# Layer 0's FFN modulation vectors on VectorE in the output projection and the first FFN, in place of TensorE in the projections

## The chip, the cores and the metric

The kernel runs on one core of a Trainium2 chip. A core has five engines with their own instruction queues: TensorE (PE, matrix multiplies; PEld is its weight load), VectorE (DVE), ScalarE (ACT), GpSimd (POOL) and SyncE (SP, which here only issues DMAs). Each queue runs in order. The metric is the device time of one execution in microseconds (us), the median of several runs.

## The reference, cut to what matters

Two layers work on 1024 latent and 256 context tokens of width 1024, all in float32. Every layer is modulated by six vectors that come from a conditioning vector, one set for the latent and one for the context tokens:

```python
sc, scc = jax.nn.silu(c), jax.nn.silu(c_ctx)
for l in range(DEPTH):
    mod_l = jnp.split((sc @ ada_w[l] + ada_b[l])[:, None, :], 6, axis=-1)
    mod_c = jnp.split(scc @ ada_w[l] + ada_b[l], 6, axis=-1)
    h_lat = rms_norm(x, norm1_g[l]) * (1 + mod_l[1]) + mod_l[0]
    ...
    x = x + mod_l[2] * y_lat
    h = rms_norm(x, norm2_g[l]) * (1 + mod_l[4]) + mod_l[3]
    x = x + mod_l[5] * conv_ffn(h, ffn_w_up[l], ffn_conv_w[l], ffn_conv_b[l], ffn_w_down[l])
    ...
```

So vectors 0 and 1 are shift and scale of the mixer, 2 is its gate, and 3, 4 and 5 are shift, scale and gate of the FFN. `ada_w[l]` is 1024 x 6144. Layer 0's mixer is attention (12 heads) beside a gated convolution of width 31 over 512 channels; layer 1's is a long convolution beside a recurrence.

## The kernel before, in words

**Layout.** Activations lie transposed: 8 tiles of 128 channels by 1280 tokens (256 context, then 1024 latent). A dense product in float32 is made as three matmuls on halves of the numbers (`mm3`, L338 to L340): high by high, high by low, low by high. Weights come in units of 128 x 1024 (`wunit`): a DMA on SP into `wraw` (2 buffers), a cast to the high part `whi` on ACT (L331), and the low part `wlo` by a subtraction on POOL (L332), 3 buffers each.

**Modulation vectors, two ways.** Layer l's `adaw` lies in three sets s of two vectors each, and a set in four quarters j of 512 columns: s = 0 holds vectors 0 and 1, s = 1 holds 2 (j = 0, 1) and 3 (j = 2, 3), s = 2 holds 4 (j = 0, 1) and 5 (j = 2, 3). `ada_gen` makes a set on TensorE: for each of 8 row blocks k a DMA brings 128 x 1024 weights (two quarters), and two matmuls with `sc` (128 x 32, of which two columns are used) as weights add them up in one psum tile `adaps`, each quarter j in its own 32 columns of the array (L365); at the end a copy, four transposes (`adapt`, L374) and the addition of the bias (L379) write `modT`. `ada_vec` makes a set on VectorE: for each quarter and k a DMA of 128 x 512, then one multiply (L395) or multiply-add (in the helper `stt`, L1197) for each of the two conditionings into the accumulator `adacc`; after 8 k, tiny matmuls with ones (`adv`, L405) add over the partitions, and the bias is added in the helper `add` (L1193). `ada_vec` is a generator that yields its booked cost, 0.7 us for each multiply-add; a `Side` object (`side`) runs such generators in turn, and `side.run(us)` puts out as many of their instructions as that budget covers.

**Order.** The program is written in one order, and a scheduler arranges each engine's queue by a simulated timeline with the order of writing as priority; `later(n)` lowers the priority of what is written in it by n instructions.

**Layer 0's projections** (`layer0`, to about 380 us). Set 0 is made first. Then come, in this order, the gated halves of the convolution input for channel blocks 0 to 3 (`l0_conv`) and the attention inputs in five blocks (`l0_block`, ten token tiles each: matmuls, then ACT, DVE and POOL work on `z` and a DMA to memory). The convolution's taps are side work: 104 multiply-adds on DVE (L1197), and 8 taps each of blocks 0 and 1 as a scaled copy on ACT into a buffer `ctap` (L722) and an accumulating DMA issued from POOL (L723), which DVE adds at the end. With `later(400)`, behind block 0 and behind block 1, the TensorE form makes the sets s = 1 and s = 2 of layer 0, and its weight tiles take their turn in the same three `ctap` buffers (the class constant `ADA` says behind which steps).

**Attention** runs to about 984 us. **The output projection** (`project`, 984 to 1150) then splits the last three of ten input chunks (`load_split`, buffers `ysrc`), and computes the 8 output blocks m first for token tiles 0 and 1 (the context and half of the latent tokens), then for tile 2; each result is scaled by the gate and added to x on DVE, its squares are summed on ACT and POOL, and after a group TensorE, DVE and POOL make the norm's factor.

**The first FFN** (`ffn` and `build`, to about 2150): `ada_A` joins scale and gain; `norm_h` normalizes on DVE, ACT and POOL; then for each of 22 blocks f `up` makes value and gate, and `side.run(8.5)` puts out side work; after every second f from 2 on, `down` adds the products of two earlier blocks to x, scaled by vector 5 (`resid`, L869 and L872). The side work is layer 1's three sets by `ada_vec` (s = 0 for both conditionings, the others for the latent tokens alone) and the long convolution's filters (`filters`). What is left is put out ahead of the last `project`.

Of the kernel before, what the change touches and what calls it, by code (L numbers as in the profile page):

```python
# [17 lines left out]
P = 128  # L18
# [229 lines left out]
class Kern:  # L248
# [129 lines left out]
        for i, j in enumerate(js):  # L378
            nc.vector.tensor_tensor(out=dst[:, j], in0=src[:, i], in1=bias[:, j], op=ALU.add)  # L379

    def ada_vec(self, l, s, cs, wbuf, acc, psf, pool=None):


        nc = self.nc
        bias = self.col(f"adab{l}", 48, 2)
        for j in range(4):
            a = [acc(i) for i in range(len(cs))]
            for k in range(KD):
                w = wbuf()
                nc.sync.dma_start(out=w, in_=self.i["adaw"][l, s, k, j // 2][:, j % 2 * 512:j % 2 * 512 + 512])  # L390
                for i, c in enumerate(cs):
                    f = self.sc[:, k, c:c + 1]
                    if k == 0 or pool:
                        t = pool() if k else a[i]
                        (nc.gpsimd if pool else nc.vector).tensor_scalar(out=t, in0=w, scalar1=f, scalar2=None, op0=ALU.mult)  # L395
                        if k:
                            self.add(a[i], a[i], t, pool=True)
                    else:
                        self.stt(a[i], w, f, a[i])
                yield 0.7 * len(cs)  # L400
            ps = psf("adv")
            n = len(cs)
            for b in range(4):
                for i in range(n):
                    nc.tensor.matmul(ps[:, b * n + i:b * n + i + 1], lhsT=a[i][:, b * P:(b + 1) * P],  # L405
                                     rhs=self.ones[:, 0:1], start=True, stop=True)
            m = slice(s * 16 + 4 * j, s * 16 + 4 * j + 4)
            self.add(self.modT[l][:, m, cs[0]:cs[-1] + 1], ps[:, :4 * n].rearrange("p (b c) -> p b c", c=n),
                     bias[:, m, cs[0]:cs[-1] + 1])
# [81 lines left out]
                    nc.vector.scalar_tensor_tensor(out=lo, in0=t, scalar=b, in1=h.bitcast(F32),  # L491
                                                   op0=ALU.add, op1=ALU.subtract)

    def project(self, weights, hs, x, l, j, tts, accs, scratch=None, cuts=(-1,)):

        K = len(hs)
        pbs = []
# [3 lines left out]
        for group in (tiles[a:b] for a, b in zip(cuts, cuts[1:])):  # L501
            ss = [accs(n)[:, :t[1][1]] for n, t in enumerate(group)]
            for m in range(KD):
# [7 lines left out]
                for n, (i, (o, N, lat)) in enumerate(group):  # L511
# [4 lines left out]
                    xt = x[m][:, o:o + N]  # L516
                    self.stt(xt, out, self.mod(l, j, m, 1 - lat), xt)
                    sq[n] = self.ss_add(ss[n], xt, m, N, scratch, m == KD - 1)
            for n, (i, (o, N, lat)) in enumerate(group):
                pb = None  # L520
                if self.ns and i < 2:
# [34 lines left out]
    def layer0(self):  # L556
# [3 lines left out]
        with ExitStack() as sa:  # L560
# [44 lines left out]
            side = Side()  # L605
            self.od = [self.dr.tile([P, T], F32, name=f"od{c}") for c in range(10)]
            zs = [None] * 5
            ada = [(0, 1), (0, 2)]
            for blk, c in ((None, 0), (None, 1), (None, 2), (4, 3), (0, None), (1, None), (2, None), (3, None)):
                if blk is not None:  # L610
                    zs[blk] = self.l0_block(blk, h, c1, side)
# [1 line left out]
                    conv[c] = self.l0_conv(c, h, c1, c2, side, ready)  # L613
                if ada and (blk, c) in self.ADA:
                    with self.later(400):
                        self.ada_set(*ada.pop(0), lambda: c2.tile([P, UL], F32, name="adaw", tag="ctap", bufs=3), self.a_ps)
        if "z" in self.dbg:
            for b in range(5):
                for i in range(2):
# [16 lines left out]
        with ExitStack() as sc:  # L636
# [8 lines left out]
                return self.wunit(self.i["wo0t"][m // 4].rearrange("p m k c -> p (m k c)"))  # L645
            tail = unit_tail(0)
            ready = [unit(0)]
            hs = early + self.load_split(oh, [self.od[k] for k in order[7:]], T, (512, TC + 512, T), 2)
            for k in range(KD):
                nc.sync.dma_start(out=x[k], in_=self.i["xT"][k])  # L650

            def weights(m):
# [9 lines left out]
                def wk(i):  # L662
                    k = order[i]
                    if k < 8:
# [3 lines left out]
                return wk  # L668
            pbs = self.project(weights, hs, x, 0, 2, self.TT,
                               lambda n: oh.tile([P, 512], F32, name="ssacc", tag="ssacc", bufs=2),  # L670
                               lambda n: oh.tile([P, 512], F32, name=n, tag="ssq", bufs=2))
        self.oc.close()
        return x, pbs

    PTAPS = (8, 8, 0, 0)
    VCUT = 1300
    DEFER = ()
    ADA = ((None, 0), (None, 1))
    RB, RV, RC = 0.75, 2.0, 12.0

    def glu(self, c, g):
# [1204 lines left out]
def build(tc, ctx, ins, out, at, dbg=None, upto=None):  # L1886
# [14 lines left out]
    with ExitStack() as s:  # L1901
# [2 lines left out]
        k.fp = k.pool("fp", stack=k.fs)  # L1904
        k.norm_h(0, 1, x, hh, hl, k.TT, pbs)
        side = Side()
        for n in range(3):
            side.add(k.ada_vec(1, n, (0,) if n else (0, 1),
                               lambda: k.st.tile([P, 512], F32, name="adaw", tag="sq", bufs=3),
# [50 lines left out]
```

## Time and profile before

| | |
|---|---|
| median of 3 runs | 3833.98 us (3825.24 to 3834.63) |
| the profiled execution | 3841.95 us, its span 3839.9 us |
| mean granted TensorE clock | 0.963 |
| busy share of the span | PE 91%, PEld 76%, DVE 59%, POOL 35%, ACT 33% |
| chain that ended last | PE 71%, DVE 12%, issue 7%, ACT 4%, DMA 4%, POOL 3% |
| modulation weights loaded | 128 DMAs of 256 KB, 32 of 512 KB |

The profile shows one execution. Its time and its span differ by what lies ahead of the first and behind the last instruction. In the page's picture of the span in 40 slices a digit is the busy share in tenths. An arrow in a list of waits points to what ended the wait, with the total, the number of times and the longest. A row of the timeline has the start, the duration, the engine, the line, the operation, what it wrote and read, and its count. A matmul on whole float32 numbers (adaps, adv) stands as two records in the trace, one on the halves (L338 to L340) as one.

### The profile page before, as it was taken

How to read it: one execution, taken by the hardware profiler on the slowest of the kernel's cores; microseconds unless marked ns; L12 is line 12 of the kernel's file. 1: busy time of each engine (PE TensorE's matmuls, PEld its weight loads, DVE VectorE, ACT ScalarE, POOL GpSimd, SP SyncE). 2: the span in 40 equal slices, each digit the busy share in tenths (PEclk: the TensorE clock that was granted, in tenths of full speed). 3: DMA queues.
4: the chain of work that ended last, by engine and by line, in shares of the span. 5: the costliest groups of instructions: out<-in, count | busy, mean ns of one | idle time of the engine just before them, and what ended most of it. 6: DMA issues, size and time to landing. Idle time of an engine off the chain costs nothing.

```text
span 3839.9 us, 48138 instructions
## 1 busy us (share of the span) xinstructions
PE 3499.0 (91%) x18708; PEld 2918.8 (76%) x18708; DVE 2281.4 (59%) x2824; ACT 1257.2 (33%) x2175; POOL 1361.1 (35%) x1024
## 2 busy tenths in 40 slices
PE   6988688888899999999999899999777889999998
PEld 4768566666787888888888788977666778888886
DVE  5978456666226656655656688355697454343435
ACT  4134566666233111222222422222111342222222
POOL 3148242211262111122332554355566642222123
PEclk9999799999999999999999899999888999999999
DMA  5374111000322223212222377523345311111111
GB/s 205 114 184 105 56 57 32 21 24 20 106 83 85 86 92 101 75 56 71 79 78 69 122 212 203 146 89 103 114 143 196 121 61 50 50 43 51 44 55 55
DMA packets 202867, 351.12 MB, mean 91 GB/s; under 512 B 23504, under 2 KB 124432, under 8 KB 202640
## 3 DMA queue, kind: packets, MB, share of 16 engines
q1 hardware_dynamic: 172240, 311.22, 25.2%
q0 software_dynamic: 26496, 30.48, 3.7%
q10 hardware_dynamic: 3904, 6.36, 0.5%
q8 instruction: 147, 2.41, 0.3%
q14 instruction: 80, 0.66, 0.1%
HBM read 275.04 MB, written 62.39 MB: 88 GB/s over the span
## 4 chain that ended last, share of the span: by engine, by line
PE 71%; DVE 12%; issue 7%; ACT 4%; DMA 4%; POOL 3%; SPq 0%; DVEq 0%; ACTq 0%; POOLq 0%
PE dl L338 13%; PE dl L339 13%; PE dl L340 13%; PE pj L338 2%; PE pj L340 2%; PE pj L339 2%; PE pT L1048 2%; PE dc L338 2%; PE dc L340 2%; PE dc L339 2%; PE o L1062 1%; DVE pl L1053 1%; PE S L1009 1%; PE S L1010 1%; PE Bp L1570 1%
## 5 line engine op out<-in xcount | busy, mean ns | idle before, releaser
L332 POOL TENSOR_TENSOR wlo<-wraw,whi 128x1024 fp32r<-128x1024 f32 (+1 forms) x226 | 575.3, 2552 | 1214.7 <-ACT whi L331 1214.3
L339 PE MATMUL dl<-hl,whi 128*128 128x512 f32 x1920 | 759.4, 396 | 4.0 <-POOL hl L1193 3.4
L338 PE MATMUL dl<-hh,whi 128*128 128x512 f32 x1536 | 604.8, 394 | 9.3 <-DVE fc L1104 7.4
L340 PE MATMUL dl<-hh,wlo 128*128 128x512 f32 x1536 | 604.0, 393 | 0.0
L331 ACT CAST whi<-wraw 128x1024 fp32r<-128x1024 f32 (+1 forms) x226 | 225.0, 1005 | 867.0 <-PE dl L339 412.9
L339 PEld LDWEIGHTS dl<-hl,whi 128*128 128x128 f32 x1920 | 363.3, 189 | 84.0 <-POOL hl L1193 5.5
L1102 DVE SCALAR_TENSOR_TENSOR fc<-dl,cols,fc 128x1023 f32<-128x1023 f32 x84 | 107.5, 1279 | 407.8 <-ACT fc L1101 407.8
L338 PEld LDWEIGHTS dl<-hh,whi 128*128 128x128 f32 x1536 | 289.9, 189 | 73.8 <-issue 7.6
L340 PEld LDWEIGHTS dl<-hh,wlo 128*128 128x128 f32 x1536 | 289.8, 189 | 65.2 <-POOL wlo L332 0.7
L872 DVE SCALAR_TENSOR_TENSOR x<-dl,modT,x 128x1024 f32<-128x1024 f32 x160 | 204.3, 1278 | 115.0 <-PE dl L340 114.0
L338 PE MATMUL dl<-gs,whi 128*128 128x512 f32 x640 | 253.9, 397 | 9.2 <-DVE fc L1104 9.2
L340 PE MATMUL dl<-gs,wlo 128*128 128x512 f32 x640 | 250.5, 391 | 0.0
L339 PE MATMUL dl<-gs,whi 128*128 128x512 f32 x640 | 250.5, 391 | 0.0
L1053 DVE TENSOR_TENSOR pl<-pT,ph 128x512 fp32r<-128x512 f32 x252 | 167.8, 686 | 74.2 <-ACT ph L1052 73.7
L1048 PE MATMUL pT<-ident,p 128*128 128x128 f32 x1008 | 166.6, 288 | 44.8 <-DVE pl L1053 39.3
L1026 DVE TENSOR_REDUCE nm<-S 128x1 f32<-128x1280 f32 (+1 forms) x120 | 153.0, 1275 | 56.0 <-PE S L1010 53.5
L1052 ACT CAST ph<-pT 128x512 fp32r<-128x512 f32 x252 | 142.5, 586 | 131.3 <-PE pT L1048 130.3
L1062 PE MATMUL o<-ph,vs 128*128 128x256 f32 x504 | 144.8, 301 | 34.3 <-ACT ph L1052 20.3
L1048 PEld LDWEIGHTS pT<-ident,p 128*128 128x128 f32 x1008 | 120.6, 146 | 69.1 <-DVE pl L1053 54.1
L1197 DVE SCALAR_TENSOR_TENSOR conv<-u,cols,conv 128x1287 f32<-128x1287 f32 (+14 forms) x104 | 172.1, 1685 | 0.9
L1193 POOL TENSOR_TENSOR ot<-ot,rb 64x256 f32<-64x256 f32 x60 | 43.5, 725 | 332.2 <-DVE ot L1193 332.2
L338 PE MATMUL dl<-hl,whi 128*128 128x512 f32 x384 | 154.6, 404 | 1.7 <-ACT whi L331 0.8
(377 smaller groups left out, 8488.5 us busy)
## 6 DMA issues: line engine op xcount, KB each, us to landing
wraw<-in_wup SPq DMA_DIRECT2D x88, 512.0 KB, 3.6
adaw<-in_adaw SPq DMA_DIRECT2D x128, 256.0 KB, 2.8
wraw<-in_wdn SPq DMA_DIRECT2D x44, 512.0 KB, 3.6
adaw<-in_adaw SPq DMA_DIRECT2D x32, 512.0 KB, 4.5
df<-in_dftf POOLq DMA_DIRECT2D x64, 256.0 KB, 4.3
wraw<-in_w1f SPq DMA_DIRECT2D x24, 512.0 KB, 3.7
x<-in_xT SPq DMA_DIRECT2D x16, 640.0 KB, 9.4
spd<-so SPq DMA_DIRECT2D x68, 128.0 KB, 2.2
```

The costliest lines, as they stand in the source:

```text
L331: nc.scalar.copy(hi[:, :cols], raw[:, :cols])
L332: nc.gpsimd.tensor_tensor(out=lo[:, :cols], in0=raw[:, :cols], in1=hi[:, :cols].bitcast(F32), op=ALU.subtract)
L338: mm(out, lhsT=lh, rhs=rh, start=first, stop=False)
L339: mm(out, lhsT=lh, rhs=rl, start=False, stop=False)
L340: mm(out, lhsT=ll, rhs=rh, start=False, stop=last)
L872: nc.vector.scalar_tensor_tensor(out=xl, in0=pl, scalar=self.mod(l, j, m, 0), in1=xl, op0=ALU.mult, op1=ALU.add)
L1026: nc.vector.tensor_reduce(out=nm[:, i:i + 1], in_=s, op=ALU.max, axis=AX.X, negate=True)
L1048: nc.tensor.transpose(pt[:, (2 * a + i) * P:(2 * a + i + 1) * P], p[:, kc * P:(kc + 1) * P], self.ident)
L1052: nc.scalar.copy(ph, pt)
L1053: nc.vector.tensor_tensor(out=pl, in0=pt, in1=ph.bitcast(F32), op=ALU.subtract)
L1062: nc.tensor.matmul(o, lhsT=vs[:, kc], rhs=x[:, a * 256:a * 256 + 256], start=(kc == 0 and j == 0), stop=(kc == nk // P - 1 and j == 1))
L1197: self.nc.vector.scalar_tensor_tensor(out=out, in0=a, scalar=s, in1=b, op0=ALU.mult, op1=op)
```

## The change

Set s = 1 is made on TensorE only for j = 0, 1 (vector 2, the mixer's gate), behind block 0. Vectors 3 and 4 (s = 1, j = 2, 3 and s = 2, j = 0, 1) are made by `ada_vec` as side work of the output projection: 6.4 us of it after each of the blocks m = 0 to 6, and all that is left after m = 7 of the first group of token tiles; its weight tiles use the three buffers `sq`, its accumulators the two `ysrc`. Vector 5 (s = 2, j = 2, 3) is made by `ada_vec` as the first side work of the FFN, ahead of layer 1's sets, with accumulators in the buffers `tot` and `w3h`.

```diff
-    def ada_vec(self, l, s, cs, wbuf, acc, psf, pool=None):
+    def ada_vec(self, l, s, cs, wbuf, acc, psf, pool=None, js=(0, 1, 2, 3)):
...
-        for j in range(4):
+        for j in js:
...
-    def project(self, weights, hs, x, l, j, tts, accs, scratch=None, cuts=(-1,)):
+    def project(self, weights, hs, x, l, j, tts, accs, scratch=None, cuts=(-1,), side=None):
...
                     sq[n] = self.ss_add(ss[n], xt, m, N, scratch, m == KD - 1)
+                if side:
+                    side.run(self.OSIDE if m < KD - 1 else 1e9)
...
-            ada = [(0, 1), (0, 2)]
+            ada = [(0, 1)]
...
-                        self.ada_set(*ada.pop(0), lambda: c2.tile([P, UL], F32, name="adaw", tag="ctap", bufs=3), self.a_ps)
+                        self.ada_set(*ada.pop(0), lambda: c2.tile([P, UL], F32, name="adaw", tag="ctap", bufs=3), self.a_ps,
+                                     js=(0, 1))
...
             ready = [unit(0)]
+            side = Side()
+            for s, js in ((1, (2, 3)), (2, (0, 1))):
+                side.add(self.ada_vec(0, s, (0, 1),
+                                      lambda: self.st.tile([P, 512], F32, name="adaw", tag="sq", bufs=3),
+                                      lambda i: oh.tile([P, 512], F32, name="adacc", tag="ysrc", bufs=2),
+                                      self.s_ps, js=js))
...
-                               lambda n: oh.tile([P, 512], F32, name=n, tag="ssq", bufs=2))
+                               lambda n: oh.tile([P, 512], F32, name=n, tag="ssq", bufs=2), side=side)
...
+    OSIDE = 6.4
...
-    ADA = ((None, 0), (None, 1))
+    ADA = ((None, 0),)
...
         side = Side()
+        bufs = (lambda: k.st.tile([P, 512], F32, name="adaw", tag="sq", bufs=3),
+                lambda i: k.fp.tile([P, 512], F32, name="adacc", tag=("tot", "w3h")[i]), k.s_ps)
+        side.add(k.ada_vec(0, 2, (0, 1), *bufs, js=(2, 3)))
```

## The prediction, made before the change was timed

> **What bounds the kernel now.** I read the slices first, then the stretches that the change touches, then what TensorE (PE) and VectorE (DVE) wait for in them.
>
> ```profile
> PE   6988688888899999999999899999777889999998
> ```
>
> A slice is 96 us. PE is busy 80% or more almost everywhere, so time is won by taking work or waits from it, unless another engine stands right behind it. Then the stretches (the layer 0 projections end near 380 us, the output projection lies from 984 to 1150, the first FFN to 2085). After the length of the stretch stand the busy times of PE, of its weight loads, DVE, ACT and POOL, then PE's granted clock, the share of the DMA engines and GB/s:
>
> ```profile
> 140.00:190.00 50.00, 50.00 (x301) 32.20 (x300) 44.68 (x30) 9.09 (x15) 4.31 (x2) 1.00 0.61 182
> ...
> 280.00:340.00 60.00, 50.99 (x390) 49.77 (x389) 55.19 (x96) 29.08 (x156) 52.69 (x39) 0.94 0.58 131
> ...
> 60.00:380.00 320.00, 300.99 (x1887) 250.42 (x1886) 255.81 (x344) 102.32 (x417) 153.09 (x115) 0.96 0.46 122
> ...
> 1000.00:1083.00 83.00, 81.46 (x429) 69.52 (x430) 12.77 (x22) 19.84 (x32) 33.33 (x21) 0.97 0.24 77
> ...
> 1160.00:2085.00 925.00, 901.57 (x4623) 758.86 (x4622) 567.82 (x659) 216.20 (x244) 223.85 (x129) 0.99 0.26 80
> ```
>
> From 140 to 190 PE is the bound alone (50.00 of 50). From 280 to 340 it has gaps, and DVE (55.19 of 60) and GpSimd (POOL, 52.69) are fuller than it (50.99). In the output projection DVE is nearly empty, in the FFN it is 61% busy, and PE is nearly full in both. The chain that ended last, and the waits of PE and DVE in the projections, name the gaps:
>
> ```profile
> 230.97 9.39 DMA acc<-ctap
> 240.51 3.60 DMA adaw<-in_adaw
> ...
> 380.58 3.84 DMA zl<-zd
> ...
> PE adaps L365 <- DMA adaw<-in_adaw: 9.0, 3, 6.9
> ...
> DVE conv L1193 <- DMA acc<-ctap: 17.2, 2, 13.3
> DVE modT L379 <- PE adapt L374: 8.4, 1, 8.4
> ```
>
> The modulation weights (adaw) share three buffers, the tag ctap, with the convolution taps that leave by accumulating DMAs. PE waits 9.0 us for adaw that finds no buffer, and DVE 17.2 us for accumulations and 8.4 us for the modulation vector.
>
> **What goes from the projections.** Set (0,2) and half of set (0,1): of 32 pairs of modulation matmuls, 24.
>
> ```profile
> L365 PE MATMUL adaps<-adaw,sc 128*32 128x512 f32 x128 | 36.6, 619 | 9.0 <-DMA adaw<-in_adaw 9.0
> ...
> 181.05 0.28 PE L340 MATMUL qkv<-whi,hl 128*128 128x256 f32 x1
> 181.17 0.28 PE L338 MATMUL qkv<-whi,hh 128*128 128x256 f32 x1
> 181.38 1.05 PE L365 MATMUL adaps<-adaw,sc 128*32 128x512 f32 x4
> 182.36 0.38 PE L339 MATMUL qkv<-wlo,hh 128*128 128x256 f32 x1
> 182.58 0.28 PE L340 MATMUL qkv<-whi,hl 128*128 128x256 f32 x1
> ...
> 192.44 0.60 PE L374 MATMUL adapt<-ident,adasb 128*128 128x128 f32 x4
> ```
>
> A pair is four records (128 records are 32 pairs). From 181.17 to 182.58 are 1.41 us, in which two qkv matmuls at their pace of 0.12 also ran: a pair costs 1.17 us. 24 x 1.17 = 28.1 us, and 0.5 for one set's four transposes. The waits of PE on adaw, 9.0 us, all belong to set (0,2), which is gone. After the longest of them PE also ran slow:
>
> ```profile
> 227.45 1.92 PE L365 MATMUL adaps<-adaw,sc 128*32 128x512 f32 x4 [6.93 <-DMA adaw<-in_adaw]
> ...
> 233.52 0.36 PE L340 MATMUL qkl<-whi,hl 128*128 128x256 f32 x1
> ...
> 230.00:232.00 2.00, 2.00 (x11) 2.00 (x11) 0.00 (x0) 0.00 (x0) 1.02 (x2) 0.50 0.35 29
> ```
>
> The 6.1 us from 227.45 to 233.52, at a granted clock of 0.50, lost 3.0 us. If PE alone set the time, the gain would be 28.1 + 0.5 + 9.0 + 3.0 = 40.6 us.
>
> DVE stands behind it. In the 320 us from 60 to 380 it is busy 255.81; the idle time that the change can shorten is the 17.2 us (eight pairs fewer stand ahead of the first tap in the buffers) and the 8.4. The rest is the wait for the first convolution input, the tail after the last tap, and waits inside the blocks, which stay. So a stage set by DVE gains at most 25.6 us. Between 25.6 and 40.6 I take **29**, near the DVE end, because the last 60 us at 55.19 of 60 are what the whole stretch would look like. The transfers that go (24 of 512 KB) only make room, on SP's queue too. What is late next is the path from the projections over ACT and DVE to z.
>
> **What is added.** Six sets of accumulation: four in the output projection (shift and scale of the FFN), two in the first FFN ahead of layer 1's (its gate). The gate of the mixer stays with TensorE. Each set is 8 loads of 256 KB on SP, 2 multiplies and 14 multiply-adds on DVE, 8 tiny matmuls on PE, one addition. The first FFN does the same for layer 1 already:
>
> ```profile
> L1197 DVE SCALAR_TENSOR_TENSOR adacc<-adaw,sc,adacc 128x512 f32<-128x512 f32 x112 | 107.7, 980 | 1.6 <-DMA adaw<-in_adaw 0.9
> ...
> L395 DVE TENSOR_SCALAR adacc<-adaw,sc 128x512 f32<-128x512 f32 x16 | 12.8, 805 | 26.7 <-PE adv L405 24.6 <-DMA adaw<-in_adaw 2.2
> ...
> 1212.13 1.84 PE L405 MATMUL adv<-ones,adacc 128*128 128x1 f32 x16
> 1213.83 0.36 PE L338 MATMUL dc<-hh,whi 128*128 128x256 f32 x1
> 1214.03 0.28 PE L339 MATMUL dc<-hl,whi 128*128 128x256 f32 x1
> ...
> PE dl L338 <- DVE fc L1104: 16.5, 9, 7.4
> ```
>
> *PE:* 1213.83 - 1212.13 is 1.70 us, and the next step is 0.20 in place of 0.12: 1.78 us a set, 6 x 1.78 = **+10.7 us**. It lies on the path, since PE is full in both stages.
>
> *DVE in the output projection:* 2 x 0.805 + 14 x 0.980 = 15.3 us a set, 61 us for four, beside 12.8 us of its own between 1000 and 1083: 74 us in 83. A set can start when the matmuls of the one before have read its accumulators. The code asks for 6.4 us of side work after each of eight blocks m and books 11.2 for a set, so a set's matmuls stand behind every second block: one set in 2 x 83/8 = 21 us, against 15.3. That hides it, barely.
>
> ```profile
> L1197 DVE SCALAR_TENSOR_TENSOR adacc<-adaw,sc,adacc x112: 735/742/2897, 1171.0 to 1583.1; 128x512 f32<-128x512 f32 x112
> ...
> 1012.89 0.69 DVE L533 TENSOR_TENSOR yl<-ysrc,yh 128x512 fp32r<-128x512 f32 x1 [0.69 <-ACT yh L532]
> ...
> 1109.83 1.54 DVE L491 SCALAR_TENSOR_TENSOR hl<-nt,modT,hh 128x512 fp32r<-128x512 f32 x1
> ...
> 1150.59 0.16 DVE L451 TENSOR_SCALAR ms<-sums 128x4 f32<-128x4 f32 x1 [6.52 <-PE sums L448]
> ...
> 1245.71 0.15 DVE L1193 TENSOR_TENSOR modT<-adv,cols 128x8 f32<-128x8 f32 x1
> 1248.03 0.47 DVE L869 SCALAR_TENSOR_TENSOR x<-dc,modT,x 128x256 f32<-128x256 f32 x1
> ```
>
> The accumulators use the buffers of the split loads (yl), taken until 1013.6, while the first set's matmuls stand behind the second block, near 1021: the first set is the likely one to hold PE. The first norm, which now waits for shift and scale, ends at 1111 and is needed when the FFN starts after 1150; it may be 39 us late for nothing. Bounds: 0, and 14 us, four times the 3.4 by which 14 multiply-adds at 0.980 exceed 14 at the shortest, 0.735. I take **+3**, nearer to the FFN, where no set holds PE.
>
> *FFN:* the gate's two sets take the place of layer 1's first two sets, which have the same form. The second of those was written at 1245.71, and the first residual addition, which now waits for it, ran at 1248.03: just in time. Behind that addition on DVE stand further ones, and PE waits for the psum that they free; a late set would cost some 2 us. Everything later in the side work moves back by two sets, 30.6 us of DVE. DVE has 357 us idle there, but PE already loses 16.5 us to it in 925; scaled by 30.6/568 that is 0.9: **+1** (0 to 7.4, the longest one wait). At its end:
>
> ```profile
> 2080.00:2120.00 40.00, 39.49 (x214) 33.40 (x212) 20.17 (x33) 14.05 (x22) 13.63 (x8) 1.00 0.17 53
> ...
> L1381 DVE TENSOR_TENSOR hfb<-hps,dec x32: 671/678/694, 1712.8 to 2067.0; 128x512 f32<-128x512 f32 x32
> ...
> L1193 DVE TENSOR_TENSOR fsd<-hfb x64: 406/424/4189, 1714.0 to 2068.7; 128x256 f32<-128x256 f32 x64
> ```
>
> The code's own costs gave the side work 22 x 8.5 = 187 us for 181; now 204 are booked, and the 17 left over, the last of four filter groups, are put out ahead of the last projection. That is 8 x (0.678 + 2 x 0.424) = 12.2 us of DVE, beside which DVE has 20 idle: **+2** (0 to 12.2).
>
> The Trainium skill speaks against the change here: "SBUF — State Buffer", section "SBUF: two separate sides", says that VectorE and GpSimd take one SBUF port pair by an exclusive lock when a VectorE instruction has two SBUF inputs. The spread of one shape from 735 to 2897 ns agrees. By that rule GpSimd's whole 33.33 us could be kept from DVE: an estimate of 4 x (14 x 0.735 + 2 x 0.805) + 12.8 + 33.3 = 94 us in 83, 11 us late, still inside the 39 that the norm has, so the sum would stay.
>
> **Sum:** -29 + 10.7 + 3 + 1 + 2 = -12.3 us. The profiled execution took 3841.95 us (span 3839.9), so 3829.7 in its terms; it stands 8 us above the median of the runs, 3833.98, and in those terms I predict **3822**.
>
> **Rivals.** *The projections stay bound by DVE and POOL.* Then only what lies where PE is full is won: eight pairs (9.4), the transposes 0.5 and the slow clock 3.0, together 12.9, against 16.7 of costs: 3838. For it speaks the row from 280 to 340; against it the 25.6 us of DVE waits that should shorten.
>
> *PE is the only bound.* All 40.6 are won and only the matmuls and 2 us are paid: -27.9, 3806. For it speaks that the chain there runs through accumulations and adaw, not through DVE's taps; against it the row from 280 to 340.
>
> *Slower: SP's queue in the output projection.* An adaw load waits at the head of SP's queue for one of three buffers, and the weight loads (wraw) queue behind it.
>
> ```profile
> wraw<-in_wo SPq DMA_DIRECT2D x16, 512.0 KB, 3.6
> ...
> 1052.74 1.06 ACT whi L331
> ...
> L332 POOL TENSOR_TENSOR wlo<-wraw,whi 128x1024 fp32r<-128x1024 f32 x9 | 21.6, 2399 | 45.4 <-ACT whi L331 45.4
> ```
>
> If PE runs dry it pays the load 3.6, the cast 1.06 and the split 2.4, 7.1 us, and 3.0 of slow clock as above; once for each of four sets 40 us: 3862. It decides when SP stands longer than the two cast weights in stock last, two blocks of 83/8 = 10.4 us. Against it: in the FFN the same two kinds of load share SP, and PE's waits there (above) are on DVE alone.
>
> **Chances.** Forecast (3813 to 3830) 0.42, DVE and POOL bound 0.25, PE bound 0.22, SP's queue 0.11. The range reaches to both same-stage rivals and their costs and leaves out SP's queue and the tails: 3805 to 3840. A measurement of this kernel can tell about 0.3% from no change, 11.5 us: faster is below 3822.5. Half of the forecast and nearly all of the PE case make 0.45 faster; the other half and the DVE case 0.44 the same; 0.11 slower.
>
> **What would show it.** Records of adaps 96 in place of 192, of adv 224 in place of 128, multiply-adds on adacc 196 in place of 112. Right: the load zl, with which the chain leaves the projections, near 352 us in place of 380.58; no wait of PE on adaw after 60 us; DVE's wait on the accumulations well below 17.2; the output projection about 10 us longer, with no PE wait on adacc beyond 3 us. Wrong: PE as idle before z as between 280 and 340 but from 190 on (DVE bound), a PE wait on wlo between 1010 and 1150 (SP's queue), or a clock of 0.50 there.

## The result, and the profile after

The changed kernel takes 3884.74 us in the median of four runs, beside 3832.07 for the kernel before on the same chip: a ratio of 1.0137, with a 95% interval of 1.0123 to 1.0151. It is 52 us slower where 12 us faster were forecast, and it lies outside the range of 3805 to 3840. The profiled execution took 3889.84 us, its span is 3888.1.

First the same stretches as in the prediction, from the changed kernel (length; busy PE, PE's weight loads, DVE, ACT, POOL; PE's granted clock, DMA share, GB/s). The last one is new: it lies between the last block of the first FFN and layer 1, and the kernel before is shown there too.

```profile
140.00:190.00 50.00, 46.41 (x298) 34.58 (x296) 49.89 (x36) 14.81 (x18) 8.61 (x7) 1.00 0.60 151
280.00:340.00 60.00, 50.66 (x375) 49.76 (x376) 54.03 (x110) 22.13 (x149) 53.17 (x36) 0.90 0.14 45
60.00:380.00 320.00, 276.93 (x1788) 248.42 (x1788) 251.96 (x363) 103.87 (x430) 174.36 (x119) 0.94 0.34 88
1000.00:1083.00 83.00, 69.12 (x391) 60.80 (x390) 63.68 (x74) 13.81 (x20) 30.34 (x17) 0.92 0.41 134
1160.00:2085.00 925.00, 902.50 (x4666) 762.03 (x4666) 541.96 (x656) 209.11 (x230) 206.51 (x112) 0.99 0.25 80
...
2140.00:2170.00 30.00, 10.36 (x19) 4.62 (x20) 15.71 (x26) 5.70 (x10) 12.29 (x14) 0.54 0.44 136
```

```profile
2140.00:2170.00 30.00, 25.41 (x93) 19.69 (x93) 14.07 (x17) 14.00 (x22) 20.12 (x14) 0.69 0.28 105
```

Three rows have changed for the worse. From 60 to 380 PE is busy 24 us less, but the stage is not shorter by as much: PE is idle instead. In the output projection PE falls from 81.46 of 83 to 69.12. Between 2140 and 2170 it is busy for 10.36 of 30 us, at a granted clock of 0.54, where the kernel before (the row by itself) had 25.41 at 0.69. In the FFN's body PE is as full as it was.

The groups of instructions show that the change did what it says: 96 records of adaps where there were 192, 224 of adv for 128, 196 multiply-adds for 112 (busy time and mean ns behind the bar).

```profile
L1207 DVE SCALAR_TENSOR_TENSOR adacc<-adaw,sc,adacc 128x512 f32<-128x512 f32 x196 | 178.0, 935 | 3.9 <-DMA adaw<-in_adaw 2.6
...
L365 PE MATMUL adaps<-adaw,sc 128*32 128x512 f32 x96 | 27.6, 619 | 0.4 <-PE adapt L374 0.4
L405 PE MATMUL adv<-ones,adacc 128*128 128x1 f32 x224 | 26.5, 240 | 0.0
```

Where the time came from is read at the stage ends of the two profiled executions, in us (the last two rows are the ends of the output projection and of the first FFN with its side work):

| | before | after | difference |
|---|---|---|---|
| zl, with which the chain leaves the projections | 380.58 | 372.61 | -8.0 |
| first matmul pj of the output projection | 983.3 | 973.3 | -10.0 |
| last sums of the output projection | 1150.1 | 1164.4 | +14.3 |
| first matmul hc of layer 1 | 2174.0 | 2227.4 | +53.4 |

So in these two executions the projections gave 8 to 10 us, the output projection took 24, and the first FFN with its end took 39. What lies behind took 5 us less. Single executions scatter by some us a stage: e1, e5 and e10 below, whose projections have the changed kernel's code, have zl at 367.0, 364.2 and 365.5, and e2 and e3, which make the sets as the kernel before does, at 379.0 and 376.1.

### The profile page after: what moved, and what is told of

Read it like the earlier page. It is cut to its first block, busy times and chain, and to the rows that moved or that the text cites. A ratio compares the mean times of both kernels' runs of the same rounds, so it can differ in the third digit from the quotient of the medians.

```text
span 3888.1 us, 48296 instructions
## 1 busy us (share of the span) xinstructions
PE 3486.3 (90%) x18704; PEld 2926.1 (75%) x18704; DVE 2332.5 (60%) x2920; ACT 1257.8 (32%) x2174; POOL 1373.8 (35%) x1024
## 4 chain that ended last, share of the span: by engine, by line
PE 66%; DVE 14%; issue 7%; DMA 6%; ACT 4%; POOL 3%; SPq 0%; DVEq 0%; ACTq 0%; POOLq 0%
PE dl L338 13%; PE dl L339 13%; PE dl L340 13%; DMA acc<-ctap 2%; PE pT L1058 2%; PE pj L338 2%; PE pj L339 2%; PE pj L340 2%; PE o L1072 2%; DVE pl L1063 2%; PE dc L338 1%; PE dc L339 1%; PE dc L340 1%; PE S L1019 1%; PE Bp L1580 1%
## 5 line engine op out<-in xcount | busy, mean ns | idle before, releaser
L332 POOL TENSOR_TENSOR wlo<-wraw,whi 128x1024 fp32r<-128x1024 f32 (+1 forms) x226 | 567.0, 2515 | 1324.4 <-ACT whi L331 1324.2
L339 PE MATMUL dl<-hl,whi 128*128 128x512 f32 x1920 | 758.4, 395 | 3.9 <-POOL hl L1203 3.3
L1207 DVE SCALAR_TENSOR_TENSOR adacc<-adaw,sc,adacc 128x512 f32<-128x512 f32 x196 | 178.0, 935 | 3.9 <-DMA adaw<-in_adaw 2.6
L1207 DVE SCALAR_TENSOR_TENSOR conv<-u,cols,conv 128x1287 f32<-128x1287 f32 (+14 forms) x104 | 170.0, 1664 | 0.8
```

The lines of the kernel that those rows point to most:

```text
L332: nc.gpsimd.tensor_tensor(out=lo[:, :cols], in0=raw[:, :cols], in1=hi[:, :cols].bitcast(F32), op=ALU.subtract)
L339: mm(out, lhsT=lh, rhs=rl, start=False, stop=False)
L1207: self.nc.vector.scalar_tensor_tensor(out=out, in0=a, scalar=s, in1=b, op0=ALU.mult, op1=op)
```

## The experiments

The time beside the kernel before is the ratio less one, times 3833 us; the intervals are those of the ratios, and 0.0010 of a ratio is 3.8 us.

| run | what is in it | ratio, 95% interval | us beside before |
|---|---|---|---|
| e1_budget | the change, FFN budget 9.5 | 1.0024 (1.0014 to 1.0034) | +9.2 |
| e2_ffn_only | the FFN's part alone | 1.0103 (1.0088 to 1.0118) | +39.5 |
| e3_out_only | the output projection's part alone | 1.0050 (1.0035 to 1.0064) | +19.2 |
| e4_proj_only | the projections' part alone | 0.9962 (0.9952 to 0.9973) | -14.6 |
| e5_spread | e1, side work spread wider | 1.0045 (1.0030 to 1.0061) | +17.2 |
| e6_interleave | e4, taps in another order | 0.9968 (0.9957 to 0.9979) | -12.3 |
| e7_no_acc | e4 without accumulated taps | 0.9927 (0.9909 to 0.9945) | -28.0 |
| e8_less_dve | e4 without 26 of DVE's taps | 0.9950 (0.9937 to 0.9963) | -19.2 |
| e9_four_blocks | e4, accumulated taps in all blocks | 0.9980 (0.9970 to 0.9990) | -7.7 |
| e10_no_split | e1 without GpSimd's split in the output projection | 1.0002 (0.9993 to 1.0012) | +0.8 |
| e11_gate_only | only vector 5 moved, budget 9.5 | 0.9996 (0.9987 to 1.0004) | -1.5 |
| e12_before_no_acc | before without accumulated taps | 0.9968 (0.9955 to 0.9980) | -12.3 |
| e13_taps44 | e4, 8 of 16 accumulated taps to DVE | 0.9980 (0.9968 to 0.9992) | -7.7 |
| e14_taps00 | e4, all 16 to DVE | 0.9972 (0.9959 to 0.9985) | -10.7 |
| e15_gate_taps44 | e11, 8 of 16 accumulated taps to DVE | 0.9990 (0.9981 to 0.9999) | -3.8 |
| e16_no_scale | e4 without GpSimd's scaling | 0.9955 (0.9939 to 0.9972) | -17.2 |
| e17_before_no_scale | before without GpSimd's scaling | 0.9988 (0.9978 to 0.9998) | -4.6 |
| e18_both_less | e8 and e16 together | 0.9923 (0.9906 to 0.9941) | -29.5 |

### The end of the first FFN: e1 and e2

```diff
# e1
-                side.run(8.5)
+                side.run(9.5)
# e2: both sets whole on TensorE, project() without side
-            ada = [(0, 1)]
+            ada = [(0, 1), (0, 2)]
-    ADA = ((None, 0),)
+    ADA = ((None, 0), (None, 1))
```

> The changed kernel with the budget of the first FFN's side work at 9.5 us a block in place of 8.5, so that 22 x 9.5 = 209 us cover the 204 that are booked and no filter group is left for the end. Theory (the filters put out ahead of the last projection cost some 45 us at the end of the FFN, since PE waits in order for a chain of DVE and a copy by DMA at each step): 35 to 45 us faster than the changed kernel, so 3840 to 3850 where the kernel before has 3832; layer 1's first projection (hc) begins within 10 us of 2185 in place of 2227. Rival (the end of the FFN is late for another reason, DVE's total load or what came late from the output projection): within 5 us of the changed kernel, 3880 to 3890. The price if theory holds: the FFN's body up to 15 us longer, as more DVE work falls into each block.

> Only the part in the first FFN: the projections make all of layer 0's sets on TensorE as the kernel before does, the output projection has no side work, and the FFN makes vector 5 once more, ahead of layer 1's sets, with the budget of 8.5 us. Theory (end of the FFN): 38 to 48 us slower than the kernel before, nearly all of it between the last down product and layer 1's first projection. The prediction's own steps (two sets of matmuls 3.6, body +1, end +2): 4 to 8 us slower. Rival (the late end needs the late norm of the output projection too): between the two, 10 to 30 us.

One unit more a block takes 43 of the 52 us away (1.0137 to 1.0024), and the FFN's part alone costs 39.5. Both came as the theory said. The changed kernel's timeline of the filters' last step on DVE (shortest, median, longest duration in ns; first and last start), whole and from 2100 us on:

```profile
L1203 DVE TENSOR_TENSOR fsd<-hfb x64: 398/418/4202, 1877.6 to 2167.8; 128x256 f32<-128x256 f32 x64
...
L1203 DVE TENSOR_TENSOR fsd<-hfb x22: 411/418/1516, 2126.7 to 2167.8; 128x256 f32<-128x256 f32 x22
```

A filter step has two fsd, so 11 steps of 32 stand behind 2100. The chain that ended last passes through them (start, length, what):

```profile
2143.15 1.74 DMA sdd<-fsd
2144.89 0.69 DVE hfb L1391
2145.60 0.77 DVE fsd L1203 x2
2146.80 2.46 DMA sdd<-fsd
2149.38 0.96 DVE fsd L1203 x2
2150.44 2.27 DMA sdd<-fsd
2152.83 1.10 DVE fsd L1203 x2
2153.98 2.32 DMA sdd<-fsd
```

And PE, in the same stretch, with its idle time before each start in brackets:

```profile
2151.29 0.80 PE L1389 MATMUL hps<-w3h,hst 128*128 128x512 f32 x1 [2.37 <-DVE hfb L1391]
2154.87 0.80 PE L1389 MATMUL hps<-w3h,hst 128*128 128x512 f32 x1 [2.36 <-DVE hfb L1391]
2158.45 0.79 PE L1389 MATMUL hps<-w3h,hst 128*128 128x512 f32 x1 [2.36 <-DVE hfb L1391]
2167.65 2.08 PE L1407 MATMUL l1b<-tot,ones 128*128 128x512 f32 x2 [7.98 <-POOL tot L1203]
```

The last of these steps come every 3.58 us: a step's fsd must wait for a buffer that a store of 2.3 us still reads. DVE is half idle meanwhile, but each step's matmuls stand in PE's queue ahead of the last projection's, and PE does nothing else.

From the last projection's first matmul pj to layer 1's first hc are 114.9 us in the changed kernel and 114.1 in e2, against 69.3 in the kernel before and 69.1 in e1. Of the 45.6 us that the changed kernel has more there, 30.6 are idle time of PE: it waits 21.1 us for the filters (hfb 7.8, hst 3.5, tot 8.0, w3h and w3l 1.8), and 10.0 for the sums of the norm behind them, which cost 4.4 before. The other 15.0 are busy time: 9.5 us of the filters' matmuls, and the rest with the granted clock at 0.76 in place of 0.85. The body ahead, from the last sums of the output projection to that pj, has lost the 11 steps and is 6.5 us shorter (954.6 to 948.1), which leaves 39.

Spread among the blocks in e1, the same steps cost little: its body takes 955.4 us. With the budget of 9.5 the last fsd starts at 2084.5 and layer 1's first hc matmul at 2182.3:

```profile
L1203 DVE TENSOR_TENSOR fsd<-hfb x64: 399/415/4202, 1787.2 to 2084.5; 128x256 f32<-128x256 f32 x64
```

What is left of the FFN's part in e1 is 9.2 + 14.6 - 19.2 = 4.6 us by the parts. By the traces it is less: from the last sums of the output projection to the first hc are 1024.5 us in e1 (1157.8 to 2182.3) and 1023.9 before. Runs of one kind differ by as much (1019.5 in e3, 1024.0 in e4, both without the gate's two sets), so no more than a few us can be said.

### The output projection: e3, e5 and e10

```diff
# e3: the sets whole on TensorE, no gate in the FFN's side work
-        side.add(k.ada_vec(0, 2, (0, 1), *bufs, js=(2, 3)))
# e5: e1 and
-                    side.run(self.OSIDE if m < KD - 1 else 1e9)
+                    side.run(self.OSIDE if gi == 0 or m < 1 else 1e9)
-    OSIDE = 6.4
+    OSIDE = 4.5
-                                      self.s_ps, js=js))
+                                      self.b_ps, js=js))
# e10: e1 and, for the weights of the output projection
+            nc.scalar.copy(lo[:, :cols], raw[:, :cols])
+            return hi, lo
```

> Only the part in the output projection: the projections as in the kernel before, the FFN as in the kernel before, and the output projection makes vectors 3 and 4 once more as side work. Theory (a set's 16 multiplies stand on DVE's queue ahead of the additions to x, so psum comes free late and PE waits): 20 to 28 us slower than the kernel before, of which 20 or more in the first group of token tiles, with PE waits on DVE's addition to x of 14 us. The prediction's own steps: 10 us slower (7.1 of it tiny matmuls). Rival (the output projection only ends late in the changed kernel because the first FFN weights or SP's queue are late): within 12 us of the kernel before.

> The kernel with the budget of 9.5 in the FFN, and in the output projection the side work at 4.5 us a block instead of 6.4, over nine blocks and the rest behind the tenth (two blocks of the second group of token tiles); the sets' tiny matmuls use another psum buffer, because the one of before is held for the norm. Theory (at 6.4 us the four sets, 44.8 us as booked, fall exactly into seven blocks, 61 us of VectorE beside 11 of its own in 73, so the additions to x come late): 8 to 14 us faster than with 6.4, 3829 to 3835; the first group's sums of squares start 10 us or more earlier against the start of the stage, and the PE waits on the addition to x fall from 14 to under 5. Rival (the cost is what PE itself does for the sets and the handing over of the accumulators): within 4 us, 3839 to 3847. Second rival (the norm, now later, holds the start of the FFN): slower than 3847, with PE idle at 1150.

> The kernel with the budget of 9.5 in the FFN; in the output projection GpSimd's split is left out of the computation: the low part of a weight tile is a copy of the whole made by ScalarE. Theory (VectorE's multiply-adds, 0.74 us each where nothing else runs, stretch up to 2.8 us while GpSimd works, and so the additions to x queued behind them come late): the multiply-adds between 985 and 1100 us take below 0.85 us in the mean where they took 1.1, PE's waits on the addition to x fall from 14 to under 6, and the kernel is 6 to 14 us faster than 3843. Rival (the waits come from the order and number of the multiply-adds alone): waits of 10 us or more, time within 4 us of 3843.

The part alone costs 19.2 us, a little under what the theory said, and PE's waits on the addition to x were 9.9 us there and not 14. In the changed kernel DVE spends from 985 to 1100 us (groups; busy time and mean ns behind the bar)

```profile
L1207 DVE SCALAR_TENSOR_TENSOR adacc<-adaw,sc,adacc 128x512 f32<-128x512 f32 x56 | 53.1, 997 | 2.4 <-DMA adaw<-in_adaw 1.9
...
L395 DVE TENSOR_SCALAR adacc<-adaw,sc 128x512 f32<-128x512 f32 x8 | 6.4, 806 | 6.3 <-PE adv L405 6.2
```

on the four sets, and its timeline there has:

```profile
1027.08 0.74 DVE L1207 SCALAR_TENSOR_TENSOR x<-pj,modT,x 128x512 f32<-128x512 f32 x1
1027.74 13.11 DVE L1207 SCALAR_TENSOR_TENSOR adacc<-adaw,sc,adacc 128x512 f32<-128x512 f32 x8
1040.77 0.74 DVE L1207 SCALAR_TENSOR_TENSOR x<-pj,modT,x 128x512 f32<-128x512 f32 x1
```

Eight multiply-adds take 13.11 us, 1.64 each, and the addition to x behind them comes late. GpSimd works in just that stretch:

```profile
1027.55 2.42 POOL L332 TENSOR_TENSOR wlo<-wraw,whi 128x1024 fp32r<-128x1024 f32 x1 [8.96 <-ACT whi L331]
1029.91 2.90 POOL L1203 TENSOR_TENSOR ssacc<-ssacc,sq 128x512 f32<-128x512 f32 x2
1032.77 2.79 POOL L332 TENSOR_TENSOR wlo<-wraw,whi 128x1024 fp32r<-128x1024 f32 x1
1037.49 2.82 POOL L332 TENSOR_TENSOR wlo<-wraw,whi 128x1024 fp32r<-128x1024 f32 x1 [1.92 <-ACT whi L331]
```

PE stands for it:

```profile
1041.66 0.55 PE L338 MATMUL pj<-och,whi 128*128 128x256 f32 x1 [7.91 <-DVE x L1207]
```

In e10 GpSimd's split is gone, and the same eight take 7.03 us in DVE's timeline (L1214 is L1207 of the changed kernel):

```profile
1024.13 7.03 DVE L1214 SCALAR_TENSOR_TENSOR adacc<-adaw,sc,adacc 128x512 f32<-128x512 f32 x8
1031.08 0.74 DVE L1214 SCALAR_TENSOR_TENSOR x<-pj,modT,x 128x512 f32<-128x512 f32 x1
```

The mean of the 56 multiply-adds falls from 0.99 (e1) to 0.87 us, a little above the 0.85 that was expected. PE's waits from 985 to 1100 are then only these two; the 14.2 us on the addition to x are gone:

```profile
PE pj L343 <- ACT yh L539: 9.4, 1, 9.4
PE pj L343 <- ACT wlo L333: 1.8, 1, 1.8
```

The kernel is 8.4 us faster than e1. So the wait needs both: multiply-adds ahead of x in the queue, and GpSimd beside them. e5 is a miss. The wait fell from 14.2 to 9.7 us only, and the stage, from its first pj to its last sums, was as long (192.2 us, 963.1 to 1155.3; e1 has 191.1, 966.7 to 1157.8). PE waits less in it and is busy 4.6 us longer (171.05 us, for 166.45 in e1). The timed difference to e1, 8 us the other way, has overlapping intervals. Its rival, a norm too late for the FFN, isn't seen: PE is busy for 10.00 of 10 us from 1150 to 1160. Why it didn't gain stays open.

### The projections: e4, e6 to e9, e12 to e14, e16 to e18

```diff
# e4: no side work in project(), no gate in the FFN, and in setup
+        nc.vector.memset(self.modT[0], 0.5)
# e6: e4 and
-        for j in pt + [j for j in taps if j not in pt]:
+        for j in order + rest[2 * max(len(pt), 1):]:    # one of pt, two others, ...
# e7: e4 and (e12: the kernel before and)
             if j in pt:
+                yield 0.3
+                continue
# e8: e4 and
-                for o in range(a, b, self.VCUT):
+                for o in range(a, b if j % 4 else a, self.VCUT):
# e9, e13, e14: e4 and
-    PTAPS = (8, 8, 0, 0)
+    PTAPS = (4, 4, 4, 4)    # e13 (4, 4, 0, 0), e14 (0, 0, 0, 0)
# e16: e4 and (e17: the kernel before and; e18: e8 and)
-                self.add(zh, zh, r.unsqueeze(2).to_broadcast([P, 4, 64]), ALU.mult, pool=True)
```

> Only the part in the projections: 24 of 32 pairs of modulation matmuls gone there, and nothing put in their place. Left out of the computation: vectors 3, 4 and 5 of layer 0, which are a constant 0.5. Theory (the stage falls back on DVE, POOL and the accumulating DMAs): 6 to 12 us faster than the kernel before, with the last load zl near 372 us, and no more. The prediction's own step: 29 us faster, zl near 352. Rival (the gain of the projections was larger in itself, and the later stages' work took it back through the order in which the scheduler writes it): 15 to 25 us faster.

> The projections alone (vectors 3, 4 and 5 of layer 0 are left out of the computation, a constant 0.5), with the taps of convolution blocks 0 and 1 in another order: one accumulated tap of ScalarE, then two of VectorE, and so on, in place of all eight accumulated taps first. Theory A (ScalarE waits in order for the accumulating DMAs, 5.2 us each one after another, and so frees psum late and holds PE; before the change the weights in the same buffers had spread these taps over 125 us): 6 to 14 us faster than the projections alone (3820.6), ScalarE's wait on the accumulations falling from 45.6 to below 20. Theory B (VectorE and GpSimd set the stage whatever ScalarE does): within 4 us of 3820.6.

> The projections alone (vectors 3, 4 and 5 of layer 0 left out, a constant 0.5), and left out as well: the 16 taps that leave by accumulating DMAs, with their copies on ScalarE and the two additions at the end on VectorE. VectorE's own 104 taps stay, at the same places. Theory A (ScalarE's wait for the accumulations holds PE): 12 to 22 us faster than 3820.6, near what the prediction gave the projections. Theory B (VectorE and GpSimd set the stage): 0 to 6 us faster.

> The projections alone (vectors 3, 4 and 5 of layer 0 left out, a constant 0.5), and left out as well: 26 of VectorE's 104 taps, some 38 us of VectorE, at the same pace of the rest. The accumulated taps stay. Theory A (ScalarE's wait for the accumulations holds PE): 0 to 6 us faster than 3820.6. Theory B (VectorE and GpSimd set the stage): 12 to 25 us faster.

> The projections alone (vectors 3, 4 and 5 of layer 0 left out of the computation, a constant 0.5), with four accumulated taps in each of the four convolution blocks in place of eight in the first two: as many on ScalarE, as many on VectorE, but the 16 accumulating DMAs lie over the whole stage. Theory A (a run of 16 accumulations at 5.2 us one after another, in which ScalarE waits and holds psum, is what the stage lost): 5 to 13 us faster than the projections alone, so a ratio to the kernel before of 0.993 to 0.995 where those had 0.9962, and ScalarE's wait on the accumulations well below 45. Theory C (it is the number of the accumulations that costs, wherever they lie, since later ones hold ScalarE ahead of the copies of z): within 4 us of 0.9962 or slower.

The part alone (vectors 3, 4 and 5 are a constant 0.5 in it) gives 14.6 us, half of the 29. My first theory was that ScalarE, waiting in order for the accumulating DMAs, holds PE. In e4's timeline of ScalarE that is seen (its lines are one higher than the changed kernel's):

```profile
223.46 1.38 ACT L733 ACTIVATE ctap<-u,cols 128x1292 f32<-128x1292 f32 x1 [4.05 <-DMA acc<-ctap]
...
229.11 1.38 ACT L733 ACTIVATE ctap<-u,cols 128x1294 f32<-128x1294 f32 x1 [3.34 <-DMA acc<-ctap]
230.39 0.20 ACT L790 ACTIVATE z<-qkv 128x64 f32<-128x64 f32 x1
```

The first copies of z come behind two such waits, and PE, at 232.99, has waited 8.06 us for them. Leaving the accumulations out (e7) gave 13.4 us more, as that theory said, and PE's wait of qkl on z falls from 23.4 us to 2.8. Another order (e6) gave nothing, and spreading them over four blocks (e9) lost 7; but neither edit lowered ScalarE's wait on the accumulations as it was meant to (48.1 and 55.4 us, for 45.6 in e4), so they decide nothing. Then came the control:

> The kernel before, with the 16 taps left out of the computation that leave by accumulating DMAs (their copies on ScalarE and the two additions at the end too). Theory A (in the kernel before PE is the bound where the accumulations run, so they cost little there, and they took the gain once the modulation weights were gone): 0 to 7 us faster than the kernel before, so that without them the change in the projections is worth 21 to 28. Theory D (the accumulations cost the kernel before as much as the changed one): 11 to 16 us faster, so that the change in the projections is worth 14 with them or without.

> The projections alone (vectors 3, 4 and 5 of layer 0 left out, a constant 0.5), with four accumulated taps in each of the first two convolution blocks in place of eight; the other eight are done by VectorE, 12 us more of it. If the accumulations cost by their number, half of 13 comes back and VectorE takes 2 of it (38 us of VectorE were worth 5): 3 to 7 us faster than 0.9962. If VectorE is the next bound at once: within 3 us of it.

> The projections alone (vectors 3, 4 and 5 of layer 0 left out, a constant 0.5), with no accumulated taps: all 120 on VectorE, 24 us more of it. If the accumulations cost by their number and VectorE has room: 5 to 11 us faster than 0.9962. If VectorE is the next bound: 0 to 10 us slower than 0.9962.

The kernel before gains 12.3 us too when they are left out (e12). Without them the change is worth 28.0 - 12.3 = 15.7 us, some 8 either way, with them 14.6: that they took the missing half of the 29 is not borne out. They cost about the same on both sides, but not by the same wait: in the kernel before it is PE's wait on adaw that is gone in e12, in e4 its waits on z are gone in e7. Taps given to DVE in their place (e13, e14) cost 7 and 4 us, with intervals that overlap e4's.

The next reading is by stretches. GpSimd's rs_r, the factor of the norm of q and k, is made once for each of the 40 token tiles of the four attention-input blocks. The timeline of the kernel before has it from 243.2 to 382.2, and adaps on PE, cut at 243:

```profile
L427 POOL TENSOR_TENSOR rs_r<-qkms,mhalf x40: 1002/1130/3412, 243.2 to 382.2; 128x4 f32<-128x4 f32 x40
...
L365 PE MATMUL adaps<-adaw,sc x76: 592/617/1062, 143.9 to 239.6; 128*32 128x512 f32 x76
...
L365 PE MATMUL adaps<-adaw,sc x52: 592/605/617, 244.2 to 276.1; 128*32 128x512 f32 x52
```

and e4's has:

```profile
L428 POOL TENSOR_TENSOR rs_r<-qkms,mhalf x40: 1001/1188/3607, 231.6 to 367.2; 128x4 f32<-128x4 f32 x40
```

Of the 96 records that go, 52, or 13 pairs and 15.2 us, lay inside the blocks, and the blocks got 3.4 us shorter (139.0 to 135.6). With the projections of before, e2 and e3 have 140.6 and 138.5; with those of the change, e1, e5 and e10 have 137.6, 135.0 and 135.8, and only the changed kernel's own profile has 143.9. The other 44, 11 pairs and 12.9 us, lay ahead, and the blocks begin 11.6 us sooner (8 to 13 by these runs). That 12.9 and 11.6 agree is in part luck: 7.4 us of PE's waits on adaw lay ahead of the blocks too and are gone, and the 8.06 us for z stand in their place. Still, what won lay ahead of the blocks. Inside them (windows of e4, and below of the kernel before) no engine is full in e4, but PE, DVE and GpSimd are all near 85%:

```profile
232.00:367.00 135.00, 114.15 (x880) 112.44 (x880) 115.20 (x242) 53.63 (x356) 112.00 (x85) 0.92 0.27 73
```

```profile
243.00:382.00 139.00, 126.64 (x941) 112.52 (x941) 114.42 (x247) 60.78 (x356) 105.83 (x90) 0.98 0.50 132
```

> The projections alone (vectors 3, 4 and 5 of layer 0 left out of the computation, a constant 0.5), and left out as well: GpSimd's scaling of q and k, 40 multiplies of 0.95 us in the four blocks. Theory G (GpSimd sets the pace of the blocks, so the 13 pairs of matmuls that went from there won nothing): the stretch from the first to the last rs_r falls from 135.6 to 125 us or less, the kernel is 8 to 16 us faster than the projections alone, and the distance to the same omission in the kernel before (the other run of this pair) grows from 14 us to 18 to 28. Rival (the pace comes from VectorE, or from the way PE, ScalarE, VectorE and GpSimd wait for one another tile by tile): within 5 us of the projections alone, and the distance stays within 11 to 17 us.

> The kernel before, with GpSimd's scaling of q and k left out of the computation, as in the other run of this pair. Theory G: PE comes to be what sets the blocks, since the 13 pairs are still there, so this gains less than the other: 0 to 7 us faster than the kernel before. Rival: as much faster as the other run is against the projections alone, within 3 us.

> The projections alone (vectors 3, 4 and 5 of layer 0 left out of the computation, a constant 0.5), with both left out: 26 of VectorE's 104 taps and GpSimd's scaling of q and k. The stretch from the first to the last rs_r was 135.6 us with both there, 127.7 without the taps, 130.9 without the scaling; PE's own matmuls in it need 40 x 24 x 0.12 = 115 us. If VectorE and GpSimd set the stretch together (one of them waits where the other works): 122 us or less, and 9 us or more faster than the projections alone (0.9962), so 0.994 or lower. If the handing over from tile to tile sets it: 126 us or more, and not below the 0.995 that leaving out the taps gave.

GpSimd alone isn't it: without its scaling the blocks take 130.9 us where 125 or less were expected, the change is worth 17.2 - 4.6 = 12.6 us, and the expectation of 18 to 28 failed. DVE alone isn't either (e8: 127.7). The intervals of e8 and e16 overlap e4's, so that these two are told by the length of the blocks and not by the time. With both relieved the blocks take 121.5 us, near PE's own 115 (40 tiles of 24 matmuls at 0.12 us), and the kernel is 15 us faster than e4, clear of the intervals, as expected if the two engines set the stretch together (timeline and window of e18):

```profile
L428 POOL TENSOR_TENSOR rs_r<-qkms,mhalf x40: 1003/1110/4670, 232.9 to 354.4; 128x4 f32<-128x4 f32 x40
```

```profile
233.00:354.00 121.00, 111.03 (x880) 110.02 (x880) 79.62 (x227) 53.69 (x359) 77.35 (x48) 0.94 0.30 81
```

The two also lengthen each other. In the blocks of e16, DVE has 244 operations as in e4, and they take 102.5 us in place of 115.7; in those of e8, GpSimd has 86 where e4 has 85, and they take 100.1 in place of 112.4.

e18 had no partner with the sets of before, so how much of the 13 pairs comes back there wasn't tried.

### Versions that might beat both: e11 and e15

```diff
# e11: e1, project() without side, set (0,2) on TensorE with js=(0, 1)
+                                     js=(0, 1, 2, 3) if ada.pop(0)[1] == 1 else (0, 1))
# e15: e11 and
-    PTAPS = (8, 8, 0, 0)
+    PTAPS = (4, 4, 0, 0)
```

> Only the FFN's gate, vector 5, is taken from TensorE: the projections make the other five vectors of layer 0, eight pairs of matmuls fewer than before; the output projection has no side work; the FFN makes vector 5 ahead of layer 1's sets at the budget of 9.5. By the parts measured so far the FFN's part costs 4 to 6 us with that budget, and the projections give a third to a half of their 14: 0 to 3 us on either side of the kernel before, 3829 to 3836. If the projections' gain comes only where the weights leave the tap buffers altogether, 4 to 6 us slower than before; if it came mostly with the first eight pairs, 4 to 8 us faster.

> The kernel that moves only the gate (e11, 0.9996), with four accumulated taps in each of the first two convolution blocks in place of eight. If the accumulations cost by their number also beside one TensorE set and a half: 3 to 7 us faster than the kernel before, 0.998 to 0.999. If not: within 3 us of it or slower.

Moving the gate alone is no different from the kernel before. With half of the accumulated taps on DVE it is 3.8 us faster, with an interval that ends at 0.9999. Among 18 runs that can be chance, and in e4 the same edit lost 7 us, so that it beats the kernel before isn't shown.

## Why the prediction was wrong, step by step

**The projections, -29.** Failed. Measured -14.6, with zl at 365.6 in e4 for 352. The step that failed was to take DVE's 25.6 us of waits for a gain near its end; 'DVE's wait on the accumulations well below 17.2' did not come, it was 22.4 us in the changed kernel. DVE's room was not its idle time: its operations and GpSimd's lengthen each other in the blocks, which got 3.4 us shorter for 13 pairs less. The rival 'the projections stay bound by DVE and POOL' had 12.9 from where PE is full, 9.4 of it for eight pairs, and came nearest; the runs have 11 pairs ahead of the blocks. I had read the row from 280 to 340 right, and then not taken it at its word. No wait of PE on adaw was left, as predicted, but an 8 us wait on ScalarE stood in its place.

**The output projection, +7.1 and +3.** Mis-sized. Measured 19.2 together by e3, 12.1 where the +3 stood, inside its bound of 14; by the changed kernel's own stage it is 24.3 - 7.1 = 17.2, beyond the bound. DVE's work was sized well: 53.1 + 6.4 = 59.5 us measured for 61. What failed is 'One set in 21 us, against 15.3. That hides it, barely': an average over 83 us, where eight multiply-adds stood ahead of one addition to x and took 13.11 us. I also named the wrong wait: no set held PE, the additions to x did. The Trainium skill's rule in "SBUF — State Buffer", section "SBUF: two separate sides", was the one that mattered: by it I had an estimate of 11 us late, and it was set aside because the norm had 39 us to spare. The norm was indeed late for nothing; x was not. e10 agrees with the rule: without GpSimd's splits the eight take 7.03 us.

**The FFN's body, +3.6 and +1.** Right as far as can be told from e1: 4.6 by the parts, 0.6 by the traces. PE's wait on DVE there is 17.1 us in the changed kernel, for 16.5.

**The FFN's end, +2, bounds 0 to 12.2.** Failed, and most of the result: 43 us by e1, 39.5 - 4.6 = 35 by e2. That booked work would be left was right; it was 11 steps and not the 8 of one group. The step that failed priced it by DVE's busy time, 12.2 us, beside DVE's idle time. Its price lies in PE's queue, where each step's matmuls stand ahead of the next projection: 45.6 us from the first pj to the first hc, of which 21.1 are PE's waits for the filters and 9.5 their matmuls.

**The rivals.** SP's queue did not happen: PE had no wait on wlo or adaw in the output projection. The slower side came by a mechanism that no rival had.

**The sum.** The parts, -14.6 + 19.2 + 39.5 = 44.1, leave 8 us of the 52, which the intervals of the four ratios together can hide. The changed kernel's profile has the blocks at 143.9 us (230.3 to 374.2) for e4's 135.6, but e1, e5 and e10 have 135.0 to 137.6 with the same code, so that belongs to this one execution. Its output projection is 24 us over before, e1's too, for e3's 18; why it is longer beside the changed projections wasn't tried.

## What to carry over

Price work that a budget leaves over as a chain in the queue of the engine that bounds the kernel, not as busy time of an engine with room. Where side work shares a queue with an operation that frees psum, look at the most that can stand ahead of it once, at the durations it has beside the other engines, not at the average. When matmuls are taken from a stage, count them by stretch: those that lie where PE isn't the bound win little.

## What the runs showed of the hardware

VectorE and GpSimd were each slower with more work on the other. VectorE's 128x512 multiply-adds took 0.735 us at the shortest; eight in a row took 13.11 us beside GpSimd's splits and 7.03 with the splits left out (e10). In the attention-input blocks the same 244 operations of VectorE took 13.2 us less where GpSimd had 40 operations fewer (e16), and GpSimd's took 12.4 us less where VectorE had fewer taps (e8; the profile's spans of GpSimd are rough). So busy time of either includes time in which it is held up, and the 85% of each in the blocks is no measure of the work it has.

How a single operation fares isn't settled. GpSimd's rs_r works on 128x4 elements and takes from 1.0 to 5.75 us. In e16 it got slower in the mean (groups of GpSimd from 225 to 385, e4 first, then e16):

```profile
L428 POOL TENSOR_TENSOR rs_r<-qkms,mhalf 128x4 f32<-128x4 f32 x40 | 61.6, 1559 | 12.0 <-DVE qkms L793 12.0
```

```profile
L428 POOL TENSOR_TENSOR rs_r<-qkms,mhalf 128x4 f32<-128x4 f32 x40 | 78.2, 1978 | 20.5 <-DVE qkms L793 20.5
```

In e17, the same omission in the kernel before, the mean is 1585 ns for 1470, so this isn't a rule.

Where PE turned idle, in the filter steps, its granted clock was lower too: 0.50 from 2150 to 2160, with PE busy for 3.67 of 10 us.
